# Two products from PSUM for the rope, and instructions sorted by when they are needed, in a two-layer streaming encoder

## The chip, the cores and the metric

The kernel runs on one core of a Trainium2 chip. The core has five engines that work side by side, each through its own instructions in a fixed order: TensorE (PE) multiplies matrices into PSUM, VectorE (DVE) and ScalarE (ACT) do elementwise work and read PSUM, GpSimd (POOL) does elementwise work between SBUF tiles, and SyncE (SP) here issues all DMAs. An instruction that waits for a semaphore holds everything behind it on its engine. The metric is the device time of one execution in microseconds.

## The reference

One step of a two-layer encoder on 512 new frames and 32 frames of running streams (544 columns in all), 1024 features, everything in float32:

```python
h = rmsnorm(x, g_attn)
z = h @ w_in                                   # q, k, v, c_q, c_kv, k_rope, two gates
q_da = rope(z[..., :o1]...), k_da = rope(z[..., o1:o2]...)   # 8 heads, two halves of 64 each
c_q = rmsnorm(...), c_kv = rmsnorm(...), k_rope = rope(z[..., o5:o6], q_pos)
o_da  = softmax(q1 k1) v - lam * softmax(q2 k2) v            # differential attention, 8 heads
o_mla = latent attention over c_kv and k_rope                # 8 heads
x = x + (gA * rmsnorm(o_da) + gB * o_mla) @ w_o
u = rmsnorm(x, g_ffn) @ w_up                                 # 2 x 2816 columns
x = x + (silu(conv(u)[:F]) * conv(u)[F:]) @ w_down           # causal width-3 convolution

def rope(x, pos):      # x1, x2: the halves of the last axis
    return concat([x1 * cos - x2 * sin, x2 * cos + x1 * sin])
```

The outputs are the two groups of frames after a last norm, and the new keys, values, latent rows and convolution rows of each layer.

## The kernel before

Activations lie transposed: features on the 128 partitions, the 544 columns along the free axis. A value that enters a matrix product is split into a high part, its cast to the type `fp32r`, and the low rest, and each product is three matmuls: high by high, high by low, low by high. The weights come as 128x1024 blocks through a ring of DMA buffers (`wf`); ACT casts the high part (`wh`), DVE takes the first half of the low part (`wl`) and POOL the second.

A layer goes through the same stages: the projections for the latent attention with its eight heads, the q, k and v units of the eight differential heads, with the attention of earlier heads, the sampled frames and the "finish" of head pairs woven between them, then the gates, the output projection, and the FFN. A q or k unit is 48 matmuls into one of two PSUM buffers (`dn`); the small products of the attention go to four other banks (`ax`).

The rotation of a head (`rope_unit`, line 724) multiplies the PSUM tile by `r` on DVE. `r` holds the norm's factor of each column, the same on all partitions. Then four DMAs swap blocks of 32 partitions into a second page `zs`; seven steps later POOL multiplies `zs` by the sine page and `z` by the cosine page, and four steps after that POOL adds the two, and the page is split for use. The shared key of the latent attention is folded first: its two halves of 64 partitions are added, after two more DMAs.

A softmax row block goes through `softmax` (line 777): a memset of masked scores, a row maximum on DVE (`sm`), an exponential on ACT, and then in `diff_norm` a few one-column operations and the normalised difference on DVE, which PE transposes (`ax<-ident,fpt`). The "finish" of a head (line 1168) multiplies its output by its norm (POOL, for the first three pairs), by its gate and by a gain (`gdc`) on DVE, adds the other attention's output, and splits the sum.

None of this is issued as it is written. `Program` (line 236) records every operation with what it depends on. Its `order` (line 322) then plays the program through with a cost for each operation (`cost`, line 294) and a delay from engine to engine (`SIGNAL`, line 221): whenever an engine is free it takes, of the operations that are ready, the one that was written first. The order that comes out is what is emitted, by the one call at line 371, so all instructions carry that line in the profile. Pages of the float32 tile `fpt` are dealt out by `Arena` (line 82), 18 of them, round robin.

Of the kernel before, what the change touches and what calls it, by code (L numbers as in the profile page):

```python
# [10 lines left out]
F32 = mybir.dt.float32  # L11
F32R = mybir.dt.float32r
AF = mybir.ActivationFunctionType
ALU = mybir.AluOpType
# [7 lines left out]
T = SP + SS  # L22
# [19 lines left out]
LOWS = 3  # L42

RING = (2, 3, 3)
FR_COLS = 57 * T
FP_COLS = 18 * T

# [34 lines left out]
class Arena:  # L82
    def __init__(self, t, n):
        self.t = t
        self.n = n
        self.free = [(0, n)]
        self.pos = 0
        self.low = n
# [23 lines left out]
    def release(self, a, w):  # L112
        out = []
        for p, q in sorted(self.free + [(a, a + w)]):
            if out and out[-1][1] == p:
                out[-1] = (out[-1][0], q)
            else:
                out.append((p, q))
        self.free = out


# [24 lines left out]
class Weights:  # L146
# [74 lines left out]
SIGNAL = {e: dict(zip(ENGINES, t)) for e, t in (  # L221
    ("tensor", (0, 230, 260, 230, 100)),
    ("vector", (235, 127, 180, 200, 60)),
    ("scalar", (240, 140, 0, 210, 60)),
    ("gpsimd", (190, 90, 90, 104, 60)),
    ("sync", (0, 0, 0, 0, 0)))}


def width(ap):
    n = 1  # L230
    for _, c in ap.ap[1:]:
        n *= c
    return n


class Program:
# [56 lines left out]

    def cost(self, i):
        eng, name, args, kw = self.ops[i]
        out = args[0]
        n = width(out)
        ptrs = sum(isinstance(kw.get(k), bass.AP) for k in ("scale", "bias", "scalar1", "scalar2", "accum_out"))
        if eng == "tensor":
            if name == "transpose" or kw["rhs"].dtype != F32:  # L300
                return max(n, 256) / 2.4 + 2.5, 0.0
            return 2 * (max(2 * n, 256) / 2.4 + 2.5), 0.0
        if eng == "sync":
            move = n * out.ap[0][1] * 4 / 360.0
            return max(475.0, move), 2100.0 + move - max(475.0, move)
        if eng == "scalar":
            return (50 if self.whole.get(args[1].tensor.name) == 0 else 93) + 93 * ptrs + n / 1.2, 0.0
        if eng == "gpsimd":
            if kw.get("op") == ALU.pow:
                return 300 + 165.0 * n, 0.0  # L310
            if name == "memset":
                return 36 + n / 1.2, 0.0
            return (137 + 2.125 * n if name == "tensor_tensor" else 120 + 3.333 * n), 0.0
        if name == "memset":
            return 8 + n / 0.96, 0.0
        if name == "tensor_reduce":
            n = width(args[1])
        elif name == "scalar_tensor_tensor":
            ptrs += isinstance(args[2], bass.AP)
        return 69 + 61 * ptrs + n / (1.92 if name == "tensor_scalar" else 0.96), 30.0 * (ptrs > 0)  # L320

    def order(self):
        n = len(self.ops)
# [8 lines left out]
        avail = {e: [] for e in ENGINES}  # L332
        for i in range(n):
            if not left[i]:
                heapq.heappush(wait[self.ops[i][0]], (0.0, i))
        out = []
        self.start = [0.0] * n
        while len(out) < n:
            best = None
            for e in ENGINES:  # L340
                w, a, t = wait[e], avail[e], free[e]
                while w and w[0][0] <= t:
                    heapq.heappush(a, heapq.heappop(w)[1])
                if not a and not w:
                    continue
                t = t if a else w[0][0]
                if best is None or t < best[0]:
                    best = (t, e)
            t, e = best
            w, a = wait[e], avail[e]  # L350
            while w and w[0][0] <= t:
                heapq.heappush(a, heapq.heappop(w)[1])
            i = heapq.heappop(a)
            hold, lat = self.cost(i)
            hold *= MARGIN.get(e, 1.0)
            self.start[i] = t
            free[e] = t + hold
            out.append(i)
            for j in succ[i]:
                f = self.ops[j][0]  # L360
                ready[j] = max(ready[j], t + hold + lat + SIGNAL[e][f])
                left[j] -= 1
                if not left[j]:
                    heapq.heappush(wait[f], (ready[j], j))
        return out
# [37 lines left out]
class Kernel:  # L403
    def __init__(self, ctx, tc, io):
# [5 lines left out]
        fpt = sb.tile([128, FP_COLS], F32, name="fpt")  # L410
        self.R = Arena(frt, FR_COLS)
        self.P = Arena(fpt, FP_COLS)
        self.wf = sb.tile([128, RING[0], 1024], F32, name="wf")
# [309 lines left out]

    def rope_unit(self, r, key, split, out=None, fold=False):
        nc = self.nc

        def evac(psum):
            z, zs = self.P.alloc(T), self.P.alloc(T)
            nc.vector.tensor_tensor(z.g(), psum, r.g(), op=ALU.mult)
            if not fold:  # L730
                return rotate(z, zs)
            for q in range(2):
                nc.sync.dma_start(zs(p0=64 * q, p1=64 * q + 64), z(p0=64 - 64 * q, p1=128 - 64 * q))

            def add():
                nc.vector.tensor_tensor(z(), z(), zs(), op=ALU.add)
                rotate(z, zs)
            self.defer(6, add)

        def rotate(z, zs):  # L740
            for q in range(4):
                nc.sync.dma_start(zs(p0=32 * q, p1=32 * q + 32), z(p0=32 * (q ^ 1), p1=32 * (q ^ 1) + 32))

            def mul():
                nc.gpsimd.tensor_tensor(zs(), zs(), self.rsin(), op=ALU.mult)
                nc.gpsimd.tensor_tensor(z(), z(), self.rcos(), op=ALU.mult)

                def fin():
                    nc.gpsimd.tensor_tensor(z(), z(), zs(), op=ALU.add)
                    zs.free()  # L750
                    if out is not None:
                        nc.sync.dma_start(out, z(p1=out.shape[0]))
                    self.have[key] = split(z)
                    z.free()
                self.defer(4, fin)
            self.defer(7, mul)
        return evac
# [484 lines left out]
    def layer_front(self, l, h, acc):  # L1242
# [5 lines left out]
        self.rate = 0.0  # L1248
        self.rcos, self.rsin = self.P.alloc(T), self.P.alloc(T)
        nc.sync.dma_start(self.rcos(), io["rope"][0])  # L1250
        nc.sync.dma_start(self.rsin(), io["rope"][1])

        cq_acc = self.acc_new()
        cqa = []
# [21 lines left out]
        self.norm_stats(cq_acc, QL, "rq", 4, 3, MLA_SCALE)  # L1276
        r = self.require("r")

        kv_acc = self.acc_new()
# [37 lines left out]
        def plain(z):  # L1317
# [3 lines left out]
            return (hi,) + krl  # L1321
        self.drive(self.kr_unit(wh, h, self.rope_unit(r, "kr", plain, io["o_kr"][l], True)))

        qz = self.qr = self.R.alloc(256)
        self.have["ql"] = self.R.alloc(512), self.R.alloc(512)
        self.rate = RATE_MLA
        for p in range(4):
            self.mla_pair(l, p, h, cqa)
        for x in cqa:
# [10 lines left out]
        for p in range(4):  # L1340
            for hh in (2 * p, 2 * p + 1):
                wh, wl = W.take((l, "q", hh))
                self.drive(self.dense(wh, wl, 0, h, self.rope_unit(r, ("q", hh), lambda z: self.split_rows(z, 0.125))))
                wh, wl = W.take((l, "k", hh))
                self.drive(self.dense(wh, wl, 0, h, self.rope_unit(
                    r, ("k", hh), lambda z, hh=hh: self.split_twice(z, lows[hh % LOWS]), io["o_dk"][l, hh])))

# [18 lines left out]
        for x in h:  # L1366
            x[0].free()
            x[1].free()
        self.cleanup = (self.have.pop("r"), qz, self.rcos, self.rsin) + sum(lows, ())

# [11 lines left out]

    def mla_pair(self, l, p, h, cqa):
        nc, W = self.nc, self.W
# [65 lines left out]
        self.drive(kn_unit(2 * p, wh, wl))  # L1450
        self.drive(self.dense(wh, wl, 5, cqa, self.rope_unit(rq, ("qr", p), lambda z: self.split_rows(z, None))))
        wh, wl = W.take((l, "qk", 2 * p + 1))
# [259 lines left out]
def pack(inputs):  # L1712
# [120 lines left out]
```

## Time and profile before

| | |
|---|---|
| time, median of 3 runs | 1917.09 us (1914.59 to 1917.48) |
| the profiled execution | 1917.5 us |
| its span, first to last instruction | 1915.7 us |
| PE busy | 1851.4 us, 97% |
| PE weight loads busy | 1814.0 us, 95% |
| DVE, ACT, POOL busy | 1251.2, 878.9, 753.3 us |
| mean granted clock of PE | 0.994 |

The span is read by stage: 0 to 36 us the start, to 290 the latent attention of layer 0, 290 to 526 its differential attention, gates and output projection, 526 to 960 its FFN; 960 to 1230, 1230 to 1468 and 1468 to 1895 the same in layer 1; the rest is the end. The stages overlap at their edges. "PE" rows are matmuls, "PEld" rows are the loads of their stationary operand. In names, `dn` and `ax` are PSUM, `frt` holds split values, `fpt` float32 pages, `sm` one-column softmax values.

### The profile page before, as it was taken

What the parts mean: (1) busy time and instruction counts of PE and PEld (TensorE: products, weight loads), DVE (VectorE), ACT (ScalarE), POOL (GpSimd) and SP (SyncE); (2) the same over time, 40 slices, a digit from 0 to 9 for tenths busy, and PEclk for the clock granted to TensorE, in tenths of its full rate; (3) what the DMA queues carried; (4) which work ended last, traced back from release to release, by engine and by line L of the source; (5) the groups of instructions that cost most, each with busy time, mean ns of one, the idle gap of its engine ahead of it and who ended that gap; (6) DMA issues with size and microseconds to landing.
All of it is one profiled execution on the core that took longest, in us unless ns stands there. A gap on an engine that the chain in (4) does not pass through costs nothing.

```text
span 1915.7 us, 37003 instructions
## 1 busy us (share of the span) xinstructions
PE 1851.4 (97%) x14244; PEld 1814.0 (95%) x14244; DVE 1251.2 (65%) x2457; ACT 878.9 (46%) x1810; POOL 753.3 (39%) x856
## 2 busy tenths in 40 slices
PE   7999999988999999999999999989899999999997
PEld 7999998988999999999999999989889999999997
DVE  6677777798747777742247677687986577777212
ACT  4455564555544444432235454654664444444322
POOL 4422636476243333312233345365653333332121
PEclk9999999999999999999999999999999999999999
DMA  4422433344352222233332225244444533333222
GB/s 154 123 79 79 142 108 117 107 141 125 95 187 88 90 90 89 89 95 117 116 121 92 92 90 157 78 144 116 124 125 128 161 89 89 89 89 88 84 88 77
DMA packets 78824, 208.40 MB, mean 109 GB/s; under 512 B 11132, under 2 KB 13880, under 8 KB 78648
## 3 DMA queue, kind: packets, MB, share of 16 engines
q1 hardware_dynamic: 78648, 206.04, 34.9%
q8 instruction: 112, 1.84, 0.4%
q14 instruction: 64, 0.52, 0.1%
HBM read 170.12 MB, written 23.62 MB: 101 GB/s over the span
## 4 chain that ended last, share of the span: by engine, by line
PE 87%; DVE 8%; issue 2%; DMA 1%; POOL 1%; ACT 1%; SPq 0%; DVEq 0%; ACTq 0%; POOLq 0%
PE dn L371 73%; PE ax L371 13%; DVE fpt L371 3%; DVE frt L371 3%; DVE sm L371 1%; POOL fpt L371 0%; DVE wl L371 0%; DMA fpt<-in_x_dram 0%; SPq L371 0%; ACT frt L371 0%; ACT fpt L371 0%; DVE ax L371 0%; DMA wf<-in_wt_dram 0%; POOL wl L371 0%; DMA fpt<-in_dk_c_dram 0%
## 5 line engine op out<-in xcount | busy, mean ns | idle before, releaser
L371 PE MATMUL dn<-frt,wh 128*128 128x272 f32 (+2 forms) x8032 | 1386.8, 291 | 12.1 <-ACT wh L371 7.2
L371 PEld LDWEIGHTS dn<-frt,wh 128*128 128x128 f32 x8032 | 1157.4, 189 | 22.0 <-ACT wh L371 7.3
L371 PE MATMUL dn<-frt,wl 128*128 128x272 f32 (+2 forms) x4000 | 849.0, 291 | 3.4 <-DVE wl L371 3.4
L371 PEld LDWEIGHTS dn<-frt,wl 128*128 128x128 f32 x4000 | 640.4, 189 | 6.7 <-DVE wl L371 3.6
L371 ACT CAST wh<-wf 128x512 fp32r<-128x512 f32 (+2 forms) x534 | 323.8, 609 | 604.3 <-PE dn L371 511.2
L371 POOL TENSOR_TENSOR wl<-wf,wh 128x512 fp32r<-128x512 f32 x242 | 320.7, 1326 | 553.5 <-ACT wh L371 533.6
L371 DVE TENSOR_TENSOR wl<-wf,wh 128x512 fp32r<-128x512 f32 (+2 forms) x290 | 211.5, 733 | 225.0 <-ACT wh L371 222.7
L371 PE MATMUL ax<-frt 128*128 128x256 f32 (+5 forms) x1164 | 228.3, 323 | 19.5 <-ACT fpt L371 12.9
L371 POOL TENSOR_TENSOR fpt<-fpt 128x544 f32<-128x544 f32 (+1 forms) x144 | 207.8, 1456 | 85.9 <-DMA fpt<-fpt 78.2
L371 DVE TENSOR_TENSOR fpt<-dn,fpt 128x544 f32<-128x544 f32 (+2 forms) x291 | 154.1, 547 | 111.0 <-PE dn L371 97.9
L371 PEld LDWEIGHTS ax<-frt 128*128 128x128 f32 (+1 forms) x1164 | 175.6, 189 | 34.8 <-ACT fpt L371 16.3
L371 DVE SCALAR_TENSOR_TENSOR fpt<-fpt,vec 128x546 f32<-128x546 f32 (+1 forms) x180 | 141.2, 785 | 47.6 <-ACT fpt L371 45.6
L371 ACT ACTIVATE fpt<-ax,sm 128x128 f32<-128x128 f32 (+4 forms) x216 | 112.3, 522 | 65.8 <-DVE sm L371 54.3
L371 ACT CAST frt<-fpt 128x544 fp32r<-128x544 f32 (+5 forms) x166 | 101.7, 622 | 50.3 <-DVE fpt L371 24.1
L371 ACT CAST frt<-ax 128x384 fp32r<-128x384 f32 (+4 forms) x186 | 71.5, 395 | 109.5 <-PE ax L371 108.6
L371 POOL COPY fpt<-cin 128x2 f32<-128x2 f32 x88 | 33.8, 384 | 202.3 <-DVE fpt L371 199.2
L371 DVE TENSOR_TENSOR frt<-fpt,frt 64x544 fp32r<-64x544 f32 (+4 forms) x120 | 99.0, 828 | 13.5 <-ACT frt L371 11.3
L371 DVE TENSOR_TENSOR frt<-ax,frt 128x384 fp32r<-128x384 f32 (+4 forms) x186 | 80.3, 446 | 37.2 <-ACT frt L371 24.7
L371 DVE TENSOR_REDUCE sm<-ax 128x1 f32<-128x128 f32 (+4 forms) x216 | 99.2, 473 | 6.7 <-PE ax L371 5.1
L371 PE MATMUL ax<-ident,fpt 128*128 128x128 f32 (+1 forms) x480 | 82.4, 279 | 18.6 <-DVE fpt L371 16.0
L371 DVE SCALAR_TENSOR_TENSOR frt<-fpt,frt 128x544 fp32r<-128x544 f32 (+1 forms) x76 | 79.1, 1040 | 24.9 <-ACT frt L371 24.0
L371 POOL CAST frt<-frt 64x32 fp32r<-64x32 f32 (+1 forms) x172 | 64.4, 378 | 55.6 <-ACT frt L371 34.6
(88 smaller groups left out, 1192.3 us busy)
## 6 DMA issues: line engine op xcount, KB each, us to landing
wf<-in_wt_dram SPq DMA_DIRECT2D x243, 512.0 KB, 3.6
fpt<-fpt SPq DMA_DIRECT2D x168, 68.0 KB, 2.7
wf<-in_wt_dram SPq DMA_DIRECT2D x16, 384.0 KB, 3.1
fpt<-in_x_dram SPq DMA_DIRECT2D x16, 272.0 KB, 3.6
out_o_dv_dram<-fpt SPq DMA_DIRECT2D x16, 272.0 KB, 2.1
out_o_dk_dram<-fpt SPq DMA_DIRECT2D x16, 272.0 KB, 4.3
xa<-fpt SPq DMA_DIRECT2D x16, 272.0 KB, 2.1
fpt<-xa SPq DMA_DIRECT2D x16, 272.0 KB, 3.6
```

Source lines behind the costliest of these rows:

```text
L371: getattr(getattr(self.nc, eng), name)(*args, **kw)
```

## The change

The rope's tables take over the factor `r`. Once `r` is there, two pages are loaded with cosine and sine and multiplied by `r` on DVE (`rope_tables`); the same is done with the other norm factor for the rotated queries of the latent attention. A unit then makes two products straight from PSUM on DVE, `y` with the sine page and `z` with the cosine page, the four DMAs swap `y` into a third page, and POOL adds. POOL's two products per unit are gone, and the last step comes seven steps after the swap is written, with no second delay. Since the swap now follows the sine product, the sine table's sign is reversed. The folded key is folded as two pages. The float32 arena grows from 18 to 21 pages (and an argument of the program's builder, `dynamic_dma_scratch_size`, is set to 8192), and a new `Aged` arena gives out the page that was freed longest ago.

The planner changes throughout: new costs, new delays, a gap after each instruction, DVE and POOL kept from overlapping where both read SBUF (`shared`), DMAs priced by one common transfer time. And it plays the program twice: a first pass, then `latest` computes backwards by when each operation must start, and the second pass takes, of the operations that are ready, the one with the earliest such time. PE keeps the written order as its rank.

```diff
-FP_COLS = 18 * T
+FP_COLS = 21 * T
...
+class Aged(Arena):
+    def alloc(self, w):
...
+                inside = s + w <= self.split if w == T else s >= self.split
+                last = max(self.back[s // 32:(s + w - 1) // 32 + 1])
+                key = (0, last, -s) if inside else (1, s if w <= T else -s, 0)
...
-MARGIN = {"vector": 1.05, "scalar": 1.05, "gpsimd": 1.05}
-    ("tensor", (0, 230, 260, 230, 100)),
-    ("vector", (235, 127, 180, 200, 60)),
+    ("tensor", (0, 38, 37, 64, 60)),
+    ("vector", (55, 0, 35, 64, 60)),
...
+GAP = {"tensor": 0.0, "vector": 18.0, "scalar": 18.0, "gpsimd": 18.0}
+PORT_TAIL = {"vector": 100.0, "gpsimd": 150.0}
...
-            if name == "transpose" or kw["rhs"].dtype != F32:
-                return max(n, 256) / 2.4 + 2.5, 0.0
+            return max(109.0, 0.4535 * n + 1.5) + 190 * part, False
         if eng == "sync":
-            move = n * out.ap[0][1] * 4 / 360.0
-            return max(475.0, move), 2100.0 + move - max(475.0, move)
+            return 2000 + n * out.ap[0][1] * 4 / 300.0, False
...
+            return 155 + 1.04 * m + (62 * ptrs if name == "scalar_tensor_tensor" else 0), len(ins) - banks > 1
...
+        return 155 + 2.22 * n, True
+
+    def latest(self, order):
...
+        for i in reversed(order):
+            e = self.ops[i][0]
+            t = min(need[i], chain) if e == "tensor" else need[i]
+            late[i] = t = t - self.cost(i)[0]
+            if e == "tensor":
+                chain = t
+            for j in self.deps[i]:
+                f = self.ops[j][0]
+                need[j] = min(need[j], t - (0.0 if e == f and e != "sync" else SIGNAL[f][e]))
+        return late
+
     def order(self):
+        late = self.latest(self.schedule(range(len(self.ops))))
+        return self.schedule([i if op[0] == "tensor" else late[i] for i, op in enumerate(self.ops)])
...
+            if e == "sync":
+                free[e] = t + 60
+                dma = max(t + 1300, dma) + width(ap) * ap.ap[0][1] * 4 / 300.0
+                end = dma + 700
+            else:
+                hold, shared = self.cost(i)
+                end = (max(t, port) if shared else t) + hold
+                if shared:
+                    port = end - PORT_TAIL[e]
+                free[e] = end + GAP[e]
...
+    def rope_tables(self, r, out):
+        for i, t in enumerate(out):
+            self.nc.sync.dma_start(t(), self.io["rope"][i])
+            self.nc.vector.tensor_tensor(t(), t(), r(), op=ALU.mult)
+
+    def swap(self, dst, src, n):
+        for a in range(0, 128, n):
+            self.nc.sync.dma_start(dst(p0=a, p1=a + n), src(p0=a ^ n, p1=(a ^ n) + n))
...
         def evac(psum):
-            z, zs = self.P.alloc(T), self.P.alloc(T)
-            nc.vector.tensor_tensor(z.g(), psum, r.g(), op=ALU.mult)
+            z, y, ys = (self.P.alloc(T) for _ in range(3))
+            nc.vector.tensor_tensor(y.g(), psum, tabs[1].g(), op=ALU.mult)
+            nc.vector.tensor_tensor(z.g(), psum, tabs[0].g(), op=ALU.mult)
...
-            def mul():
-                nc.gpsimd.tensor_tensor(zs(), zs(), self.rsin(), op=ALU.mult)
-                nc.gpsimd.tensor_tensor(z(), z(), self.rcos(), op=ALU.mult)
...
-                self.defer(4, fin)
-            self.defer(7, mul)
+            def fin():
+                nc.gpsimd.tensor_tensor(z(), z(), ys(), op=ALU.add)
...
+            self.defer(7, fin)
```

What this does to the order is seen best in the differential attention of layer 0, where the first finished pair and the softmax of a later head meet. On DVE, `fpt<-fpt 128x544`, `gdc` and `gdc,oms` are the sums of a head's finish, `sm<-ax` the row maxima of score tiles. Before:

```order
L371 SCALAR_TENSOR_TENSOR fpt<-fpt 128x544
L371 MEMSET ax_97 64x64
L371 MEMSET ax_95 64x64
L371 SCALAR_TENSOR_TENSOR fpt<-fpt,gdc 128x512
L371 SCALAR_TENSOR_TENSOR fpt<-fpt,gdc,oms 128x32
L371 SCALAR_TENSOR_TENSOR fpt<-fpt 128x544
L371 TENSOR_REDUCE sm<-ax_97 128x1
L371 SCALAR_TENSOR_TENSOR fpt<-fpt,gdc 128x512
L371 TENSOR_TENSOR frt<-fpt,frt 128x544
L371 SCALAR_TENSOR_TENSOR fpt<-fpt,gdc,oms 128x32
L371 MEMSET ax_98 64x64
L371 TENSOR_REDUCE sm<-ax_95 128x1
```

And after, in the same place:

```order
L449 TENSOR_REDUCE sm<-ax_96 128x1
L449 TENSOR_TENSOR frt<-ax_98,frt 128x384
L449 RECIPROCAL sm<-sm 128x1
L449 TENSOR_TENSOR wl<-wf,wh 128x512
L449 RECIPROCAL rs<-sm 128x1
L449 TENSOR_TENSOR wl<-wf,wh 128x512
L449 MEMSET ax_95 64x64
L449 TENSOR_REDUCE sm<-ax_95 128x1
L449 MEMSET ax_96 64x64
L449 TENSOR_REDUCE sm<-ax_96 128x1
L449 RECIPROCAL rs<-sm 128x1
L449 SCALAR_TENSOR_TENSOR fpt<-fpt 128x544
```

The finish sums, which stood between the row maxima, now begin behind them.

On ACT at that place, `fpt,sm<-ax` are the exponentials and `frt<-fpt 128x544` the casts of finished heads. Before:

```order
L371 ACTIVATE fpt,sm<-ax_96,sm 128x128
L371 COPY fpt<-ax_98 128x128
L371 CAST frt<-fpt 128x544
L371 ACTIVATE fpt,sm<-ax_97,sm 128x128
L371 CAST frt<-fpt 128x512
L371 CAST frt<-fpt 128x544
L371 ACTIVATE fpt,sm<-ax_98,sm 128x256
```

After:

```order
L449 ACTIVATE fpt,sm<-ax_96,sm 128x128
L449 CAST wh<-wf 128x512
L449 ACTIVATE fpt,sm<-ax_95,sm 128x256
L449 CAST wh<-wf 128x512
L449 ACTIVATE fpt,sm<-ax_96,sm 128x384
L449 CAST wh<-wf 128x512
L449 ACTIVATE fpt,sm<-ax_97,sm 128x128
L449 CAST wh<-wf 128x512
L449 COPY fpt<-ax_98 128x128
L449 CAST wh<-wf 128x512
L449 ACTIVATE fpt,sm<-ax_97,sm 128x384
L449 CAST frt<-fpt 128x544
```

The casts of the finish moved from behind the first exponential to behind the fifth.

On POOL, `fpt<-fpt 128x544` are the rope's products and sums and the finish's first product, up to the split of a cached block (`frt<-fpt,frt`). Before:

```order
L371 TENSOR_TENSOR fpt<-fpt 128x544
L371 CAST frt<-frt 64x32 x2
L371 TENSOR_TENSOR fpt<-fpt 128x544 x2
L371 CAST frt<-frt 64x32 x2
L371 TENSOR_TENSOR wl<-wf,wh 128x512
L371 TENSOR_TENSOR fpt<-fpt 128x544 x2
L371 TENSOR_TENSOR wl<-wf,wh 128x512
L371 TENSOR_TENSOR fpt<-fpt 128x544
L371 TENSOR_TENSOR frt<-fpt,frt 128x4x128
```

After:

```order
L449 TENSOR_TENSOR fpt<-fpt 128x544 x2
L449 TENSOR_TENSOR wl<-wf,wh 128x512
L449 TENSOR_TENSOR fpt<-fpt 128x544
L449 CAST frt<-frt 64x32 x2
L449 TENSOR_TENSOR wl<-wf,wh 128x512
L449 TENSOR_TENSOR fpt<-fpt 128x544
L449 CAST frt<-frt 64x32
L449 TENSOR_TENSOR frt<-fpt,frt 128x4x128
```

The pair of rope products between the two weight splits is gone; the single sum stays. Over the whole program POOL's instructions of this form go from 140 to 56, DVE's `fpt<-dn,fpt 128x544` from 115 to 157 and its `fpt<-fpt 128x544` products and sums from 2 to 12, SP's DMAs from 654 to 662; PE's 14178 are the same by form.

## Rows read from the trace of the kernel before

**Rows 1.** The page's first part: busy us, share of the span, instructions.

```profile
PE 1851.4 (97%) x14244; PEld 1814.0 (95%) x14244; DVE 1251.2 (65%) x2457; ACT 878.9 (46%) x1810; POOL 753.3 (39%) x856
```

**Rows 2.** By stage: us; busy PE, PEld, DVE, ACT, POOL; PE clock, DMA share, GB/s.

```profile
0.00:36.00 36.00, 23.93 (x132) 22.29 (x133) 22.20 (x28) 14.99 (x24) 16.78 (x16) 0.91 0.56 175
36.00:290.00 254.00, 251.28 (x1888) 243.13 (x1887) 181.46 (x409) 132.90 (x318) 102.00 (x117) 1.00 0.34 106
290.00:526.00 236.00, 218.48 (x1633) 208.96 (x1632) 186.31 (x420) 126.32 (x304) 134.92 (x134) 0.99 0.38 117
526.00:960.00 434.00, 433.69 (x3472) 433.46 (x3471) 243.09 (x380) 170.65 (x270) 131.75 (x167) 1.00 0.33 107
960.00:1230.00 270.00, 267.17 (x2007) 259.39 (x2006) 183.60 (x411) 137.05 (x324) 105.24 (x120) 0.99 0.34 107
1230.00:1468.00 238.00, 220.17 (x1647) 210.98 (x1645) 190.18 (x422) 126.28 (x305) 131.19 (x134) 0.99 0.40 116
1468.00:1915.70 447.70, 436.68 (x3478) 435.74 (x3477) 244.39 (x391) 170.71 (x270) 131.45 (x168) 0.99 0.33 100
```

**Rows 3.** PE's waits in 290 to 526: us in total, times, longest.

```profile
PE ax L371 <- ACT fpt L371: 7.4, 7, 2.1
PE ax L371 <- DVE fpt L371: 6.9, 5, 3.2
PE ax L371 <- DVE frt L371: 1.5, 1, 1.5
```

**Rows 4.** Timeline of PE: start, us, instruction, idle before and what ended it.

```profile
330.09 0.30 PEld L371 LDWEIGHTS ax<-frt 128*128 128x128 f32 x2 [2.28 <-ACT fpt L371]
330.10 0.74 PE L371 MATMUL ax<-frt 128*128 128x512 f32 x2 [2.06 <-ACT fpt L371]
...
399.24 0.62 PE L371 MATMUL ax<-frt 128*128 128x384 f32 x2 [1.31 <-ACT fpt L371]
...
472.93 0.47 PE L371 MATMUL ax<-ident,fpt 128*128 128x128 f32 x1 [1.36 <-DVE fpt L371]
```

**Rows 5.** Timeline of POOL and DVE before 330.

```profile
324.78 3.44 POOL L371 TENSOR_TENSOR fpt<-fpt 128x544 f32<-128x544 f32 x2
...
325.13 1.88 DVE L371 TENSOR_TENSOR frt<-fpt,frt 128x544 fp32r<-128x544 f32 x1
...
326.93 1.34 DVE L371 SCALAR_TENSOR_TENSOR fpt<-fpt,gdc,oms 128x32 f32<-128x32 f32 x1
```

**Rows 6.** Timeline of DVE and ACT before 399.

```profile
396.53 0.28 DVE L371 TENSOR_REDUCE sm<-ax 128x1 f32<-128x128 f32 x1
...
397.67 0.65 ACT L371 CAST frt<-fpt 128x544 fp32r<-128x544 f32 x1 [3.35 <-DVE fpt L371]
...
398.74 0.36 ACT L371 ACTIVATE fpt<-ax,sm 128x128 f32<-128x128 f32 x1
```

**Rows 7.** Groups by form: busy us, mean ns, idle before; the first two of 290:526.

```profile
L371 DVE SCALAR_TENSOR_TENSOR frt<-fpt,frt 64x544 fp32r<-64x544 f32 x12 | 17.0, 1414 | 0.5 <-ACT frt L371 0.2
L371 DVE TENSOR_TENSOR fpt<-dn,fpt 128x544 f32<-128x544 f32 x24 | 17.1, 712 | 4.7 <-PE dn L371 4.3 <-PE ax L371 0.2
...
L371 DVE SCALAR_TENSOR_TENSOR fpt<-fpt 128x546 f32<-128x546 f32 x44 | 31.8, 722 | 0.0
L371 POOL TENSOR_TENSOR fpt<-fpt 128x544 f32<-128x544 f32 x140 | 204.8, 1476 | 82.6 <-DMA fpt<-fpt 78.2 <-DVE frt L371 2.8
```

**Rows 8.** The chain in order of time: a piece of the FFN.

```profile
571.93 392.64 PE dn L371 x3144
```

**Rows 9.** Two stretches of 4 us, columns as in rows 2.

```profile
472.00:476.00 4.00, 3.07 (x14) 2.98 (x15) 3.26 (x11) 1.51 (x5) 2.91 (x6) 0.57 0.36 93
1360.00:1364.00 4.00, 4.00 (x23) 3.94 (x22) 2.66 (x6) 2.26 (x6) 2.43 (x5) 0.59 0.85 239
```

**Rows 10.** SP's timeline: the swap of one rope unit.

```profile
395.24 2.41 SPq L371 DMA_DIRECT2D fpt<-fpt  x4
```

**Rows 11.** A stretch of 20 us, columns as in rows 2.

```profile
400.00:420.00 20.00, 15.18 (x115) 14.34 (x115) 19.83 (x41) 11.78 (x31) 15.03 (x14) 1.00 0.33 94
```

More of the change, by code (lines that the diff above doesn't have):

```diff
@@ L119, in release, with __init__ @@
         self.free = out
+class Aged(Arena):
+    def __init__(self, t, n, split):
+        super().__init__(t, n)
+        self.split = split
+        self.clock = 0
+        self.back = [0] * (-(-n // 32))
+    def alloc(self, w):
+        best = None
+        for i, (a, b) in enumerate(self.free):
+            if w == T:
+                spots = range(-(-a // T) * T, b - w + 1, T)
+            else:
+                spots = {max(a, min(self.split, b - w)), b - w} if b - a >= w else ()
+            for s in spots:
+                inside = s + w <= self.split if w == T else s >= self.split
+                last = max(self.back[s // 32:(s + w - 1) // 32 + 1])
+                key = (0, last, -s) if inside else (1, s if w <= T else -s, 0)
+                if best is None or key < best[0]:
+                    best = (key, i, s)
+        if best is None:
+            raise MemoryError(f"arena: {w} of {self.free}")
+        _, i, s = best
+        a, b = self.free[i]
+        self.free[i:i + 1] = [(p, q) for p, q in ((a, s), (s + w, b)) if q > p]
+        self.low = min(self.low, sum(q - p for p, q in self.free))
+        return Page(self, s, w)
+    def release(self, a, w):
+        self.clock += 1
+        for c in range(a // 32, (a + w - 1) // 32 + 1):
+            self.back[c] = self.clock
+        super().release(a, w)
 class Page:
@@ L297, in cost @@
         n = width(out)
-        ptrs = sum(isinstance(kw.get(k), bass.AP) for k in ("scale", "bias", "scalar1", "scalar2", "accum_out"))
         if eng == "tensor":
-            if name == "transpose" or kw["rhs"].dtype != F32:
-                return max(n, 256) / 2.4 + 2.5, 0.0
-            return 2 * (max(2 * n, 256) / 2.4 + 2.5), 0.0
+            if name == "matmul" and kw["rhs"].dtype == F32:
+                return 2 * max(109.0, 0.907 * n + 1.5), False
+            part = name == "matmul" and kw["lhsT"].ap[0][1] < 128
@@ new lines, in cost @@
+        wide = [x for x in ins if width(x) > 1]
+        ptrs = len(ins) - len(wide) if wide else 0
+        banks = sum(self.whole.get(x.tensor.name) == 0 for x in wide)
+        m = max([n] + [width(x) for x in wide])
+        if eng == "vector":
+            if name == "memset":
+                return 45 + n / 0.96, False
+            if name == "reciprocal":
+                return 155 + n / 0.96, False
+            if name == "tensor_scalar":
+                return (155 + 1.04 * m if banks else 220 + 0.52 * m), len(wide) > banks
+            if name == "tensor_reduce":
+                return 155 + 1.04 * m, False
+            if not wide:
+                return (215 if name == "scalar_tensor_tensor" else 155 + 1.04 * m), True
+            return 155 + 1.04 * m + (62 * ptrs if name == "scalar_tensor_tensor" else 0), len(ins) - banks > 1
@@ L360, in order @@
                 f = self.ops[j][0]
-                ready[j] = max(ready[j], t + hold + lat + SIGNAL[e][f])
+                ready[j] = max(ready[j], end + (0.0 if f == e and e != "sync" else SIGNAL[e][f]))
                 left[j] -= 1
                 if not left[j]:
-                    heapq.heappush(wait[f], (ready[j], j))
+                    heapq.heappush(wait[f], (ready[j], rank[j], j))
         return out
@@ L722, in split_twice, with rope_unit @@
         return (first, second) + lows
[L724 removed]
+    def rope_tables(self, r, out):
[5 more added lines that the diff above has]
+            self.nc.sync.dma_start(dst(p0=a, p1=a + n), src(p0=a ^ n, p1=(a ^ n) + n))
+    def rope_unit(self, tabs, key, split, out=None, fold=False):
@@ L1326, in layer_front @@
         self.rate = RATE_MLA
+        rotq = self.P.alloc(T), self.P.alloc(T)
+        self.rope_tables(self.require("rq"), rotq)
         for p in range(4):
-            self.mla_pair(l, p, h, cqa)
+            self.mla_pair(l, p, h, cqa, rotq)
+        for x in rotq:
+            x.free()
         for x in cqa:
```

99 lines of the change are left out of this document (48 added, 51 removed).

## The prediction, made before the changed kernel had run

> **What bounds the kernel now.** The page's first part [rows 1] gives TensorE (PE) 1851.4 us of a span of 1915.7, so 64.3 us is all it was seen idle. Its instructions are the same before and after (14178 matmuls and transposes of the same shapes, counted in both orders), so a gain can come only from that idle time, from what stalls hide inside "busy", and from a reduced clock. The table by stage [rows 2] says where it lies: 12.1 us in the first 36 (the inputs arrive), 2.7 up to 290, 17.5 in 290 to 526, 0.3 in the first FFN, 2.8 in 960 to 1230, 17.8 in 1230 to 1468, and 11.0 from there to the end, the second FFN and the last norm. The two differential-attention stages, 474 us together, hold 35.4 us, over half. There VectorE (DVE) is busy 186 of 236 and 190 of 238 us, and GpSimd (POOL) 135 and 131.
>
> PE's waits in the first of them [rows 3] are for the softmax: 7.4 us for ACT's exponentials, 6.9 for DVE's normalised rows, the longest 3.2. One by one on PE's timeline, seven of these twelve are over 1 us, together 11.7; [rows 4] has the first, the third and the last of the seven. What DVE and ACT did just before is the point of this prediction.
>
> - At 328, DVE reaches the reductions of two score tiles only after a low split of 1.88 us and a 32-column sum of the head finish of 1.34 [rows 5]. As many columns from PSUM take 0.71 [rows 7], so about 2 us of it is waiting, while POOL runs two products of the rope from 324.78 on [rows 5]. PE then waits 2.06.
> - At 397, ACT has stood idle for 3.35 us at a cast of the head finish that waits for DVE. A score tile's reduction ends at 396.81; its exponential, behind that cast and a weight cast, starts at 398.74 [rows 6]. PE waits 1.31.
>
> So the bound is an in-order queue with the wrong thing at its head, made worse by DVE and POOL getting in each other's way.
>
> **DVE and POOL.** Where both of DVE's inputs lie in SBUF the row is long in this stage: 64x544 splits take 1414 ns on the mean, a 128x546 form of the FFN 722; where one lies in PSUM it is short, 712 [rows 7]. [...]
>
> **The change, part by part.** The profiled execution took 1917.5 us, 1.8 above its span and 0.4 above the median of the runs, 1917.1; the sum starts there.
>
> 1. Rope. POOL loses 84 products at 1476 ns, 124 us of its 753; DVE gains 42 products from PSUM at 712 (30 us) and 10 operations between SBUF pages, eight for the tables and two for the folded key, near the 722 of such a form (7 us) [rows 7]. At most 16 of the products per layer lie in a differential stage: 11.4 us on a DVE with 50 us free there. The chain from PSUM to the rotated page loses two POOL products and gains one DVE product, 2.95 less 0.71, but the program now defers its last step by 7 steps, not 7 and then 4, so it does not reach the scores with more slack. Cost on PE's path: nothing while DVE's order hides it; if that cover fails, the second rival prices it. Eight more DMAs (four tables, four of the folded key) stand in SP's queue in the first 100 us of a layer; behind the start PE is idle for under 3 us there: nothing.
>
> 2. Order. The sort now goes by latest start, with costs that are nearer the rows: a 272-column matmul is priced 124.9 ns, where the trace has 392.64 us for 3144 of them, 124.9 [rows 8]; before it was 115.8. The order of after moves what it should: five exponentials stand ahead of ACT's first cast of the head finish where one did, and on DVE the finish sums stand behind the reductions. I take the seven waits over 1 us as removed and the smaller ones as kept: 11.7 per stage, and as much in the second, whose idle time is the same within 0.3: −23.5. Weight loads show each such gap 0.22 longer than matmuls do (2.28 against 2.06 [rows 4]), so 14 × 0.22 = −3.1 more. Bounds: none of it, or all 35.4 and the same 0.22 on some 30 waits, −42.
>
> 3. Clock. [...] Lost: 0.43 × 4 and 0.41 × 4, 3.4. Bounds 0 and −3.4; half, −1.7.
>
> 4. The latent-attention stretches idle 2.7 and 2.8 us: half goes, −2.8 (bounds 0 and −5.5). The head's DMAs and splits change places; its 12.1 us may move by 4 either way, taken at 0. The tail's last rows are the same on every engine: 0.
>
> 5. New waits. PE's own order is fixed by the plan, and the plan now lets SP issue a DMA every 60 ns, where before it took 475. The trace has four rope swaps on SP for 2.41 us, 0.60 each [rows 10]. A q or k page can thus be up to 4 × 0.54 = 2.2 us later than planned, and POOL, in order, holds its next weight split behind the sum that waits for it (it waited 78.2 us for swaps before [rows 7]). With 16 differential heads the upper end is +35, the lower 0; the waits of this kind that the old order left (DVE splits of q and k in front of scores) are few, 1.5 us [rows 3], so I take the low part: +5.5.
>
> Sum: 1917.5 − 23.5 − 3.1 − 1.7 − 2.8 + 5.5 = 1891.9, say 1892.
>
> **Rivals.** All waits go. For it: DVE is idle 50 us of each stage, so everything fits if sorted well. Then 1917.5 − 42 − 3.4 − 5.5 = 1867 at best, 1874 with some new waits. Against it: nothing in the plan knows which of DVE and POOL gets to read first.
>
> DVE stays the bound. For it: in 400 to 420 it is busy 19.83 of 20 [rows 11], and the products from PSUM join that queue. If only half the waits go (−13.3 with the hidden part), the other stretches give −1.4, the products that fall into such stretches (taken as two of 20 us in 236, 11.4 × 40/236 = 1.9 per layer) add 3.9 and the new waits 5.5: 1912. Against it: what POOL gives back in waiting is of the same size as those products, and over the whole stage DVE has 50 us to spare.
>
> Scores come late (the slower side). One mechanism: SP's issue time under-planned, PE standing at the first score matmul of each head with other matmuls behind it. At the full 2.2 us for each of 16 heads: 1917.5 − 31.1 + 35 = 1921. It decides from 1.94 us a head. Against it: the issues of a q or k unit overlap with the landing of the first of them.
>
> The sort does nothing where it matters, within 4 us of 1917. The order shows otherwise in the two places above; what speaks for it is that the first FFN's 434 us hold 0.3 to win, and the other's hardly more.
>
> **Chances.** Forecast (1880 to 1904) 0.55; all waits go 0.14; DVE stays the bound 0.17, of which 0.12 is more than 0.2% (3.8 us, about what a measurement tells from nothing) below the median; late scores 0.09, of which 0.08 slower by that much; no effect 0.05. Faster 0.81, within 0.2% 0.10, slower 0.09. The range 1870 to 1912 takes in the forecast, most of the deeper case, and most of the DVE case.
>
> **What would show it.** Right: PE idle of the differential stages (now 17.5 and 17.8) at 5 to 10 each, PE's waits for ACT's exponentials and DVE's normalisation down to a third, POOL's 544-column products at 56, DVE's 64x544 splits in those stages well under 1414 ns, products from PSUM near 712, FFN unchanged. Wrong: waits of PE for DVE or ACT splits of q and k in front of a head's first scores, idle time in the FFN stages, or DVE at 19.8 of 20 in the same places with PE still short of matmuls.

## The result and the profile after

| | before | after |
|---|---|---|
| median of 4 runs each | 1917.28 us | 1897.31 us (1896.69 to 1903.84) |
| ratio, 95% interval | | 0.990 (0.987 to 0.993) |
| the profiled execution, its span | 1917.5, 1915.7 us | 1903.8, 1902.1 us |
| PE idle: span less PE busy | 64.3 us | 47.2 us |
| mean granted clock of PE | 0.994 | 0.992 |

The change is 20 us faster by the medians, 5 us short of the forecast of 1892. The profiled execution of after is the longest of its four; what follows accounts for its 13.7 us.

The page's first part, after (engine, busy us, share of the span, instructions), answers to [rows 1]:

```profile
PE 1854.9 (98%) x14244; PEld 1815.9 (95%) x14244; DVE 1260.4 (66%) x2509; ACT 881.5 (46%) x1810; POOL 650.2 (34%) x772
```

The stages after, with the columns of [rows 2]: us; busy PE, PEld, DVE, ACT, POOL; clock, DMA share, GB/s. Their ends are moved with the work.

```profile
36.00:290.00 254.00, 252.02 (x1874) 244.24 (x1873) 184.94 (x410) 129.25 (x309) 71.70 (x97) 0.99 0.34 105
290.00:516.00 226.00, 218.44 (x1645) 208.55 (x1644) 181.77 (x442) 128.59 (x308) 96.31 (x109) 1.00 0.41 130
516.00:946.00 430.00, 430.00 (x3440) 430.00 (x3439) 246.14 (x379) 169.39 (x265) 142.09 (x170) 1.00 0.32 106
946.00:1230.00 284.00, 281.67 (x2110) 272.66 (x2108) 199.08 (x441) 141.75 (x335) 83.00 (x104) 0.99 0.34 107
1230.00:1454.00 224.00, 211.72 (x1570) 201.78 (x1569) 180.37 (x419) 123.02 (x296) 94.92 (x109) 0.98 0.41 126
1454.00:1902.10 448.10, 437.32 (x3476) 436.10 (x3476) 243.40 (x390) 171.13 (x269) 142.96 (x169) 0.99 0.31 97
```

PE idles 7.6 us in the first differential stage (17.5 before) and 12.3 in the second (17.8), 2.0 and 2.3 in the latent stretches (2.7 and 2.8), nothing in the first FFN, 10.8 from 1454 to the end (11.0). The idle time fell where it was expected to, in the second stage by a third only. PE's waits there (total us, times, longest), first 290 to 516, against [rows 3]:

```profile
PE ax L449 <- ACT fpt L449: 2.4, 3, 1.1
...
PE ax L449 <- DVE fpt L449: 0.7, 1, 0.7
```

The second stage, first in the kernel before, 1230 to 1468:

```profile
PE ax L371 <- ACT fpt L371: 6.7, 5, 3.0
PE ax L371 <- DVE fpt L371: 5.9, 3, 3.0
PE ax L371 <- DVE frt L371: 3.6, 4, 1.4
```

And after, 1230 to 1454:

```profile
PE ax L449 <- ACT fpt L449: 4.3, 3, 2.5
PE ax L449 <- DVE frt L449: 3.8, 5, 1.4
```

The first stage's waits for exponentials fell from 7.4 to 2.4 us, those for normalised rows from 6.9 to 0.7. In the second, those for normalised rows fell from 5.9 to 0.4, but exponentials still cost 4.3 of 6.7, and DVE's splits as much as before (3.8 and 3.6). The longest of each of these two kinds is seen on the timeline (start, us, instruction, idle before and its releaser), picked rows of SP, POOL, ACT, DVE and PE in order of time:

```profile
1340.85 1.70 DVE L449 TENSOR_TENSOR frt<-fpt,frt 64x544 fp32r<-64x544 f32 x1
...
1342.59 0.56 DVE L449 TENSOR_TENSOR frt<-ax,frt 128x384 fp32r<-128x384 f32 x1
...
1343.29 0.41 PE L449 MATMUL ax<-frt 128*128 128x128 f32 x2 [1.43 <-DVE frt L449]
...
1397.29 1.37 POOL L449 TENSOR_TENSOR fpt<-fpt 128x544 f32<-128x544 f32 x1 [5.80 <-DMA fpt<-fpt]
...
1402.62 1.82 POOL L449 TENSOR_TENSOR fpt<-fpt 128x544 f32<-128x544 f32 x1
...
1404.47 0.80 SPq L449 DMA_DIRECT2D fpt<-om  x2
...
1405.36 0.38 SPq L449 DMA_DIRECT2D wf<-in_wt_dram  x1
...
1408.88 0.29 DVE L449 TENSOR_REDUCE sm<-ax 128x1 f32<-128x128 f32 x1
...
1410.26 1.14 ACT L449 CAST wh<-wf 128x512 fp32r<-128x512 f32 x2 [2.62 <-DMA wf<-in_wt_dram]
...
1411.30 0.36 ACT L449 ACTIVATE fpt<-ax,sm 128x128 f32<-128x128 f32 x1
...
1411.80 1.66 PE L449 MATMUL ax<-frt 128*128 128x512 f32 x5 [2.48 <-ACT fpt L449]
```

At 1341 a key's split took 1.70 us in place of the 0.71 of its like at 1338.42, while POOL's split of a weight block ran from 1340.13 to 1341.97, and the split of softmax rows that PE wanted stood behind it. At 1408.88 the first score tile is reduced, at 1409.17 done; but ACT stands for 2.62 us at a cast whose weights are late, because SP issued that load only at 1405.36, behind two loads of the other attention's output (`om`). Those had held SP for 4.9 us until POOL was done with a page, at 1404.44, and POOL had itself stood 5.80 us for a rope swap, up to 1397.29. Four exponentials queue behind the cast, and PE waits 2.48. The granted clock then fell to half of full speed (0.50 in 1413 to 1415), for most of four microseconds:

```profile
1412.00:1416.00 4.00, 4.00 (x17) 3.76 (x16) 2.03 (x6) 2.12 (x8) 0.81 (x1) 0.57 0.00 0
```

Groups by form (busy us, mean ns, idle before), 290 to 516, against [rows 7]:

```profile
L449 DVE TENSOR_TENSOR fpt<-dn,fpt 128x544 f32<-128x544 f32 x36 | 24.8, 715 | 2.4 <-PE dn L449 2.2
...
L449 DVE SCALAR_TENSOR_TENSOR frt<-fpt,frt 64x544 fp32r<-64x544 f32 x12 | 9.9, 822 | 0.4
```

And over the whole program:

```profile
L449 POOL TENSOR_TENSOR fpt<-fpt 128x544 f32<-128x544 f32 x56 | 79.6, 1425 | 119.7 <-DMA fpt<-fpt 100.3 <-DMA fpt<-rd 7.8 <-PE dn L449 5.7
```

Products from PSUM still take 715 ns, the 64x544 splits fell from 1414 to 822, POOL's 544-column products are 56 for 140. All three had been named as signs. The experiments show that they do not prove what the sum claimed.

### The profile page after: what moved, and what is told of

Same layout as the page of the kernel before. It is cut to its first block, busy times and chain, and to the rows that moved or that the text cites. A ratio compares the mean times of both kernels' runs of the same rounds, so it can differ in the third digit from the quotient of the medians.

```text
span 1902.1 us, 36957 instructions
## 1 busy us (share of the span) xinstructions
PE 1854.9 (98%) x14244; PEld 1815.9 (95%) x14244; DVE 1260.4 (66%) x2509; ACT 881.5 (46%) x1810; POOL 650.2 (34%) x772
## 5 line engine op out<-in xcount | busy, mean ns | idle before, releaser
L449 PE MATMUL dn<-frt,wh 128*128 128x272 f32 (+2 forms) x8032 | 1389.0, 292 | 13.7 <-ACT frt L449 9.5
L449 PEld LDWEIGHTS dn<-frt,wh 128*128 128x128 f32 x8032 | 1157.1, 189 | 25.0 <-ACT frt L449 10.3
L449 DVE TENSOR_TENSOR wl<-wf,wh 128x512 fp32r<-128x512 f32 (+2 forms) x290 | 201.4, 695 | 181.8 <-ACT wh L449 181.0
L449 DVE TENSOR_TENSOR fpt<-dn,fpt 128x544 f32<-128x544 f32 (+2 forms) x333 | 179.4, 569 | 127.0 <-PE dn L449 113.4
L449 DVE SCALAR_TENSOR_TENSOR fpt<-fpt,vec 128x546 f32<-128x546 f32 (+1 forms) x180 | 141.2, 786 | 47.7 <-ACT fpt L449 44.5
L449 POOL TENSOR_TENSOR fpt<-fpt 128x544 f32<-128x544 f32 (+2 forms) x60 | 82.2, 1375 | 122.1 <-DMA fpt<-fpt 100.3
L449 DVE TENSOR_REDUCE sm<-ax 128x1 f32<-128x128 f32 (+4 forms) x216 | 103.4, 483 | 9.5 <-PE ax L449 4.1
L449 POOL COPY fpt<-cin 128x2 f32<-128x2 f32 x88 | 45.6, 518 | 142.6 <-DVE fpt L449 139.1
L449 DVE SCALAR_TENSOR_TENSOR frt<-fpt,frt 128x544 fp32r<-128x544 f32 (+1 forms) x76 | 83.7, 1102 | 12.7 <-ACT frt L449 11.8
L449 ACT ACTIVATE fpt<-fpt,vec 128x546 f32<-128x546 f32 x88 | 74.4, 845 | 26.3 <-DVE fpt L449 26.3
```

What stands on the lines that cost most here:

```text
L449: getattr(getattr(self.nc, eng), name)(*args, **kw)
```

## Experiments

The theory was the prediction's: the order carries the gain, the rope costs and brings nothing. The rival: the rope carries it. "Before" ran beside every group, at 1916.3 to 1916.9. Idle is span less PE busy; lost clock is (1 − mean clock) × span, which counts what falls into idle time too; both of the profiled execution. The mean clock of 23 executions of before lies between 0.989 and 0.995, 10 to 21 us of lost clock, so only the rows near 30 and above stand clear of the others in that column.

| kernel (label) | us, median | ratio to before, 95% | idle | lost clock |
|---|---|---|---|---|
| before | 1917 | | 64.3 | 11.5 |
| after | 1897.3 | 0.9868 to 0.9933 | 47.2 | 15.2 |
| arena alone (arena_only) | 1924.2 | 1.0024 to 1.0045 | 65.3 | 13.4 |
| rope and arena (rope_only) | 1900.8 | 0.9908 to 0.9933 | 49.6 | 13.3 |
| planner alone (order_only) | 1939.7 | 1.0108 to 1.0136 | 70.8 | 32.9 |
| planner and arena (order_arena) | 1933.9 | 1.0072 to 1.0121 | 66.4 | 29.0 |
| planner, SP priced (order_sp) | 1941.9 | 1.0105 to 1.0161 | 70.8 | 36.9 |
| planner, overlap (overlap_order_only) | 1913.3 | 0.9972 to 1.0002 | 47.7 | 13.4 |
| after, unsorted (costs_no_sort) | 1942.0 | 1.0112 to 1.0143 | 72.9 | 40.8 |
| the same, SP priced (no_sort_sp) | 1939.6 | 1.0101 to 1.0143 | 72.8 | 34.8 |
| the same, overlap (overlap_no_sort) | 1931.2 | 1.0051 to 1.0091 | 61.3 | 28.9 |
| after, old costs, sorted (old_costs_sort) | 1891.1 | 0.9848 to 0.9890 | 44.2 | 9.4 |
| after, SP priced (sp_real) | 1891.3 | 0.9855 to 0.9885 | 38.7 | 11.3 |
| the same, overlap (overlap_sp) | 1890.5 | 0.9828 to 0.9875 | 37.6 | 17.1 |

**The parts alone.** rope_only is after with `cost`, `SIGNAL`, `MARGIN` and `order` of before; order_only is before with those of after; arena_only is before with

```diff
-FP_COLS = 18 * T
+FP_COLS = 21 * T
-        self.P = Arena(fpt, FP_COLS)
+        self.P = Aged(fpt, FP_COLS, FP_COLS - 2 * T)
```

and with the class `Aged` and the builder's argument of after; order_arena is order_only with the same edit.

> The change's rope (products from PSUM, tables with the factor, 21 pages, aged arena) with the planner of before. Theory: the gain of 20 us is the sort's, so without it PE still waits for exponentials and normalised rows behind the head finish: 1912 to 1921 us, PE idle 15 to 19 us in each differential stage. Rival (the rope's relief of POOL and the shorter time in which DVE and POOL exclude each other carries it): 1897 to 1905, DVE's 64x544 splits below 1200 ns.

> The changed planner (costs, delays, sort) on the rope, the tables and the 18-page arena of before. Theory: the sort carries nearly all, 1896 to 1904, waits for exponentials and normalised rows at a third or less. Rival (the rope carries it): 1910 to 1917, because POOL still reads SBUF for 124 us more and the reductions stay late.

> The kernel before with the larger, aged arena alone (21 pages), its own rope and planner. If the rope carries what rope_only gained (15.5 us): 1913 to 1919. If the arena carries it: 1900 to 1906.

> The changed planner and the changed arena (21 pages, aged) on the rope of before, issue price 60. Theory A (issue price): 1932 to 1942, as without the arena. Theory B (arena): 1900 to 1917. Theory C (other costs): 1932 to 1942.

The theory fell, and the rival's figure for order_only was too mild; arena_only came out above both of its ranges. Against before, in us, all four with 21 pages: arena +7.2; arena and rope −15.5; arena and planner +17.5; all, −20.0. So the rope is worth −22.7 under the old planner and −37.5 under the new, and the planner +10.3 on the old rope and −4.5 on the new. Added, the three would be −5.2, and together they are −20.0: with these costs the planner needs the rope. The larger arena costs 7.2 by itself and saves 5.8 under the changed planner (order_only against order_arena).

The rope takes away the very waits that the prediction gave to the order. PE's waits for normalised rows and for exponentials over the whole trace of arena_only:

```profile
PE ax L409 <- DVE fpt L409: 18.9, 20, 2.3
PE ax L409 <- ACT fpt L409: 11.8, 11, 2.1
```

And of rope_only, which has the same planner and arena:

```profile
PE ax L409 <- DVE fpt L409: 7.8, 12, 1.5
PE dn L409 <- DVE fpt L409: 7.8, 9, 2.0
...
PE ax L409 <- ACT fpt L409: 6.0, 10, 1.7
```

From 30.7 to 13.8 us, where the idle time went from 65.3 to 49.6. In return PE waits 7.8 us for DVE to have read a PSUM buffer (`dn`), which now takes two products; in arena_only that is 0.6.

DVE's own work became shorter. The window of rope_only, 290 to 516 (columns as above):

```profile
290.00:516.00 226.00, 213.71 (x1606) 205.30 (x1605) 178.83 (x425) 124.34 (x301) 94.62 (x107) 0.99 0.39 125
```

Its groups by form there:

```profile
L409 DVE TENSOR_TENSOR fpt<-dn,fpt 128x544 f32<-128x544 f32 x36 | 25.2, 716 | 6.0 <-PE dn L409 5.4
...
L409 DVE SCALAR_TENSOR_TENSOR frt<-fpt,frt 64x544 fp32r<-64x544 f32 x12 | 9.4, 783 | 0.4
```

The window of arena_only, 290 to 526:

```profile
290.00:526.00 236.00, 220.68 (x1646) 210.47 (x1645) 185.65 (x421) 126.37 (x304) 128.95 (x131) 0.99 0.39 121
```

And one of its groups:

```profile
L409 DVE SCALAR_TENSOR_TENSOR frt<-fpt,frt 64x544 fp32r<-64x544 f32 x12 | 11.0, 919 | 0.5 <-ACT frt L409 0.2
```

The 64x544 splits are a poor sign: in arena_only they are nearly as short, and the kernel is slower than before. DVE's whole stage says more. Without the products from PSUM, before has 186.3 − 17.1 = 169.2 us [rows 2, 7], arena_only 185.65 − 17.1 = 168.6, rope_only 178.83 − 25.2 = 153.6, after 181.77 − 24.8 = 157.0, over about the same work. With 40 us less of POOL in the stage, DVE's other work is 12 to 16 us shorter; the added products cost 8. In the trace of before, all 19 of the 84 64x544 splits of the whole program that took over 1 us ran beside POOL instructions and ended 0.58 to 0.59 us after the end of one of them; the five that met none took 0.72. In after it is 21 of 84, again 0.58 to 0.59 us behind, and the 23 that met none took 0.71 to 0.72. One of before's:

```profile
338.50 1.29 POOL L371 TENSOR_TENSOR wl<-wf,wh 128x512 fp32r<-128x512 f32 x1 [0.23 <-POOL frt L371]
...
338.83 1.54 DVE L371 SCALAR_TENSOR_TENSOR frt<-fpt,frt 64x544 fp32r<-64x544 f32 x1
```

From PSUM it is otherwise: in before 103 of DVE's 146 128x544 products and sums with `dn` ran beside POOL, and none took over 0.73 us. That DVE's splits stop waiting for POOL fits the shorter work, as it fits the splits of [rows 5]; no run kept POOL's products and took only the contention away, so it is not shown apart from POOL's shorter queue and from the two POOL products that are gone between PSUM and the rotated page. Nor does DVE's busy time set the kernel's: overlap_no_sort (below) has the least of all, 1233.9 us, and takes 1931.2.

**Why the planner alone loses.** order_only idles 6.5 us more than before, and its PE is busy for 15.2 us longer with the same instructions, at a mean clock of 0.983. In its timeline (picked rows of SP, POOL, ACT and PE) a swap's four DMAs stand apart:

```profile
317.41 1.15 SPq L411 DMA_DIRECT2D fpt<-fpt  x2
...
320.83 1.15 SPq L411 DMA_DIRECT2D fpt<-fpt  x2
...
326.09 12.39 POOL L411 TENSOR_TENSOR fpt<-fpt 128x544 f32<-128x544 f32 x8 [5.06 <-DMA fpt<-fpt]
...
330.52 0.37 ACT L411 ACTIVATE fpt<-ax,sm 128x128 f32<-128x128 f32 x1 [2.80 <-POOL fpt L411]
...
337.19 1.74 ACT L411 CAST frt<-fpt 128x544 fp32r<-128x544 f32 x3 [2.04 <-POOL fpt L411]
...
341.56 0.74 PE L411 MATMUL ax<-frt 128*128 128x512 f32 x2 [2.36 <-ACT fpt L411]
```

POOL stands 5.06 us, then runs eight products in a row, ACT's queue waits for them twice, and PE behind ACT. Behind these waits the clock is at 0.50 throughout 346 to 350 (window, order_only):

```profile
346.00:350.00 4.00, 3.20 (x15) 3.22 (x16) 3.79 (x8) 2.33 (x6) 2.16 (x2) 0.50 0.42 135
```

The price of a DMA issue was the first suspect (order_sp and no_sort_sp, and with the sort sp_real):

```diff
-                free[e] = t + 60
+                free[e] = t + (600 if ap.ap[0][1] <= 64 else 450)
```

> The changed planner on the rope and 18-page arena of before, a DMA issue priced at 600 ns (32- and 64-row swaps) or 450 in place of 60. With 60 the four DMAs of a swap stood apart in SP's queue (317.41 and 320.83), POOL stood 5.06 us and then ran eight products in a row to 338.45, with DVE's and ACT's finish held up and PE waiting. Theory A (the issue price does this): 1905 to 1918, POOL's long waits for swaps gone. Theory B (18 pages, dealt round robin, tie the order): 1932 to 1942. Theory C (the other new costs and the short delays from engine to engine): 1930 to 1942.

It falls: 1941.9, and 1939.6 unsorted (no_sort_sp, below). The pages are not it either: they give back 5.8 of the loss (order_arena, above). Two runs asked whether the sort or the costs are at fault; costs_no_sort has `order` return `self.schedule(range(len(self.ops)))`, old_costs_sort the prices of before with `latest` and two passes:

> The changed kernel with its new costs and delays but played once, written order as the rank of every engine. Theory (the sort itself): the finish sums and casts stand in front of reductions and exponentials again, 1910 to 1920. Rival (the better costs are what counts, the sort little): 1896 to 1903.

> The changed kernel played once in written order, a DMA issue priced at 600 or 450 ns. Theory A (the issue price made the unsorted order slow, 1942): 1898 to 1912, near the old planner with the new rope, 1900.8. Theory C (the other new costs made it slow): 1930 to 1942. If both count, between, and the sort then brings the rest down to the 1891 of the sorted order at the same price.

> The changed rope and arena with the costs and delays of before (a DMA issue at 475) and the two passes with the sort. Theory A (sort good, the issue price of 60 bad): 1888 to 1896. Theory C' (the sort lives from the new costs): 1900 or above, no better than the old order's 1900.8.

The sort is good: −9.7 with the old costs, −44.7 with the new. The new costs are bad: +41.2 unsorted (costs_no_sort is slower than both of its ranges), +6.2 sorted. The 9.7 do not lie in the softmax waits, which are 13.8 us in rope_only and 14.7 in old_costs_sort: in the profiled executions, which are 11.2 us apart, 5.4 are other idle time and 5.8 are PE's busy time. Sort and old costs on the old rope were not run. Singly, the new costs are closer to the trace. What they miss is seen where a queue is full. Timeline of after, first DVE, then ACT:

```profile
402.09 0.72 DVE L449 TENSOR_TENSOR fpt<-dn,fpt 128x544 f32<-128x544 f32 x1
402.73 0.41 DVE L449 TENSOR_TENSOR frt<-ax,frt 128x256 fp32r<-128x256 f32 x1
403.06 0.74 DVE L449 SCALAR_TENSOR_TENSOR fpt<-fpt,gdc 128x512 f32<-128x512 f32 x1
...
1397.26 0.62 ACT L449 CAST wh<-wf 128x512 fp32r<-128x512 f32 x1
1397.78 0.69 ACT L449 ACTIVATE fpt<-ax,sm 128x512 f32<-128x512 f32 x1
```

An instruction of 0.72 us is followed after 0.64, one of 0.41 after 0.33, one of 0.62 on ACT after 0.52: the next starts before the last has ended, by some 0.1 us. On DVE 322 of the 380 instructions that wait for no semaphore start 60 to 100 ns before the end of the last; of the 656 that wait for that one itself, 509 start 20 to 40 ns after its end. The new costs are whole durations with a gap of 18 ns behind, so the plan takes DVE for busier by 0.1 us for each instruction of a full queue. The old ones put that part into the delays between engines. The edit:

```diff
-GAP = {"tensor": 0.0, "vector": 18.0, "scalar": 18.0, "gpsimd": 18.0}
+GAP = {"tensor": 0.0, "vector": -82.0, "scalar": -97.0, "gpsimd": -49.0}
```

with 34, 32 and 59 ns from an instruction of DVE, ACT and POOL to a dependent one on the same engine. They were taken from the gaps between neighbouring instructions in after's trace: on DVE these gather near −80 and near 35 ns, on ACT near −100 and near 25, on POOL near −50 and near 60.

> order_only (1939.7 us: the changed planner on the rope and the arena of before) with the overlap edit, issue price 60. Theory D (the planner's fault alone): 1895 to 1912, about 15 behind the same planner on the new rope. Rival (84 more POOL products leave the sort no room, whatever the prices): 1925 or above.

> costs_no_sort (1942 us) with one edit in the planner: an engine is free again before its instruction ends, by 82 ns on DVE, 97 on ACT, 49 on POOL, where nothing depends (in after's trace DVE starts at 402.09, 402.73, 403.06 after durations of 0.72, 0.41); dependent ones follow 32 to 59 ns after the end. The changed planner added 18 ns after each in place of this. Theory D (the plan fails because it takes DVE and ACT for busier than they are, by some 0.1 us for each of 2509 and 1593 instructions): 1900 to 1918. Rival (the rest of the new costs, such as PE at 124.9 ns a matmul or the short delays): 1930 to 1942.

On the old rope this is the whole loss: 1939.7 to 1913.3, just outside the theory's range and no longer told from before; idle 70.8 to 47.7, lost clock 32.9 to 13.4. POOL's timeline at the same place in overlap_order_only:

```profile
321.13 3.12 POOL L411 TENSOR_TENSOR fpt<-fpt 128x544 f32<-128x544 f32 x2 [0.63 <-DMA fpt<-fpt]
324.21 1.29 POOL L411 TENSOR_TENSOR wl<-wf,wh 128x512 fp32r<-128x512 f32 x1
```

The eight in a row are gone. Unsorted it brings 10.8 of the 41.2: 1931.2 lies in the rival's range, not the theory's, and the other 30 stay open; the price of a matmul (124.9 for 115.8 ns) and the shorter delays were not tried alone.

**The waits that are left.** In after itself:

> The changed kernel, its planner pricing a DMA issue on SP at 600 ns for 32- and 64-row swaps and 450 ns for others in place of 60. Theory (the new waits of the first scores for splits of q and k, 4.3 us for DVE's and 1.5 for ACT's splits in the whole trace of after, come from swaps that land later than planned): these waits halve, 1893 to 1896. Rival (they come from DVE and POOL holding each other up, not from SP): 1896 to 1900, the waits as they were. Second rival: the plan gets worse elsewhere, above 1900.

1891.3, below all three, and the executions do not meet (1887.9 to 1895.3 against 1896.7 to 1903.8). PE's waits in sp_real's second differential stage, 1218 to 1442:

```profile
PE ax L449 <- DVE frt L449: 0.5, 1, 0.5
PE ax L449 <- ACT fpt L449: 0.2, 1, 0.2
```

From 3.8 and 4.3 to 0.5 and 0.2; the wait at 1411 is gone. POOL too waits less for swaps, 69.2 us where after has 100.3:

```profile
L449 POOL TENSOR_TENSOR fpt<-fpt 128x544 f32<-128x544 f32 x56 | 79.2, 1417 | 94.2 <-DMA fpt<-fpt 69.2 <-DVE sm L449 8.0 <-PE dn L449 6.3
```

With the sort and the new rope the issue price does matter. It orders SP's queue otherwise; that the load at 1405.36 above was late through this price alone is not shown.

> The changed kernel with the issue price of sp_real (1891.3 us) and the same overlap edit, sorted. Theory D: 1868 to 1884, fewer waits of PE in the differential stages and a mean granted clock of at least 0.994. Rival (the sort has already made the plan sound, and what is left is neither): 1888 to 1895.

1890.5, in the rival's range: with the sort and the SP price, the overlap changes nothing that can be measured. With the overlap in the plan, the new rope (overlap_sp) is 22.8 us faster than the old (overlap_order_only), about the 22.7 that it is worth under the old planner, though these two kernels differ in the arena and the SP price as well. So what the 37.5 above are more than 22.7 seems to come from costs that failed on the old rope, and not from sorting as such. By their medians old_costs_sort, sp_real and overlap_sp are each some 6 us faster than after; they are not told apart.

## Why the prediction was right or wrong

The time was near (1897.3 for 1892, within 1880 to 1904), and that was luck: what the sum gave to the order the rope brought, and the rope stood in it at nothing.

1. Rope: taken as "Cost on PE's path: nothing". This step failed. With the larger arena under both, it is −22.7 under the old planner, the largest term. The price of the products was right (715 for 712 ns). What was not valued is what POOL's 84 missing products give back: in the rival on DVE it was put at "the same size as those products", 11.4 us at most in a stage; the products added 8 us, and DVE's other work lost 12 to 16.
2. Order: −23.5 − 3.1. Failed in its cause. The waits went as said in the first stage, but rope_only, with the old order, already idles only 49.6 of before's 64.3, where after has 47.2. The sort brings 9.7 with the old costs; the new costs take 6 of them back here and, on the old rope, turn the whole to a loss. "Costs that are nearer the rows" was the wrong inference: nearer as durations, not as occupancy of a queue.
3. Clock, −1.7: wrong sign in the profiled execution. The 3.4 it is half of stand in [rows 9], (1 − 0.57) × 4 and (1 − 0.59) × 4; no run shows the half. In its place (1 − clock) × span goes from 11.5 to 15.2, and PE's busy time, with the same instructions, rises by 3.5. The two falls of [rows 9] are gone, but two others stand behind waits that are left (1.43 us up to 1343.29, 2.48 up to 1411.80; 0.57 in 1344 to 1348 and in 1412 to 1416), and one came without a wait (258 to 266, last section). Over more executions the sign is open: after's four have a clock of 0.992 to 0.994, well within before's.
4. Latent stretches, −2.8: −1.2, and nothing lost in the head, the FFN or the end, as said.
5. New waits, +5.5: right in the root and, by sp_real, in size (its issue price takes 6.0 off, and 31 us off POOL's waits for swaps). The way to PE was longer than the one named: a late swap held POOL, POOL a page, the page SP's queue, and so a weight load, ACT's cast and the exponentials. PE waited for these and for splits of softmax rows, not for q and k.

Added up for the profiled execution: 15.4 less idle in the differential stages, 1.2 in the latent ones, 3.7 more clock: −12.9 of its −13.7. The arena, which the sum does not price, costs 7.2 alone.

## What to carry to other kernels

A change of two halves is predicted half by half, and each is worth a run: here planner and rope were +10 and −23 apart, with an arena of +7, and all three together −20 where the sum is −5. A planner that gives out instructions one by one wants two prices for each, how long it keeps its queue and when its result is there; one exact duration used for both was worse here than a rough occupancy with a generous delay (+41.2 unsorted, +6.2 sorted). Putting the occupancy right brought 26.4 us on the old rope, 10.8 on the new one unsorted, and nothing measurable once sort and SP price were there. Work taken off POOL is not to be put at nothing because POOL is idle half the time; look for what DVE and PE wait for while POOL is busy.

## What the runs showed of the hardware

Some long waits were paid twice, others not. In before PE waited 3.05 us up to 1358.48, and the clock was 0.59 in 1360 to 1364; it waited 3.20 us up to 416.09, and the clock was 1.00 in 416 to 420. order_only, with only 6.5 us more idle time than before, lost 32.9 us of clock for 11.5; one of its falls is that in 346 to 350, behind waits, 0.50.

The clock also fell without a long wait. In after PE ran 32 matmuls of 32 columns in a row, and while they ran the clock fell from 1.00 (258 to 258.5) to 0.50 (259 to 265), with PE busy all the time (timeline):

```profile
256.15 4.59 PE L449 MATMUL ax<-fpt 128*128 128x32 f32 x32
```

The windows there:

```profile
258.00:262.00 4.00, 4.00 (x24) 4.00 (x24) 1.26 (x3) 0.62 (x1) 0.14 (x1) 0.61 0.82 288
262.00:266.00 4.00, 4.00 (x22) 3.94 (x21) 1.55 (x6) 1.85 (x6) 0.00 (x0) 0.54 0.07 26
```

The kernel before has the same behind its 32 in layer 1 (1199.32, 3.65 us):

```profile
1202.00:1206.00 4.00, 4.00 (x24) 3.93 (x24) 2.51 (x6) 2.02 (x5) 0.90 (x2) 0.61 0.36 132
```

Not each time: behind those of its layer 0 (259.33, 3.65 us) the clock stayed at 1.00 (259 to 268). From 250 to 266 in after PE was in no wait that could have been removed, and the prediction's term for the clock counts only the two falls of [rows 9].
